# Fifteen instead of twelve gate halves queued among the banded steps of a hybrid decoder block

## The chip, the cores and the metric

The kernel runs on one core of a Trainium2 chip. The metric is the device time of one execution in microseconds. Engines are named as in the profile: PE (TensorE matmuls), PEld (its weight loads), DVE (VectorE), ACT (ScalarE), POOL (GpSimd) and SP (SyncE, which issues nearly all transfers here).

## The reference, cut to what matters

One decoder block on x of 1024 tokens by 1024 columns, in float32. Two attention branches work on the same normed input, each is weighted by a sigmoid gate, and their sum goes on through an output product and a squared-ReLU MLP.

```python
proj = jnp.einsum('bld,de->ble', h, w_in[l])
a_q, a_k, a_v, i_q, i_k, i_w, b_q, b_k, b_v, g_a, g_b = jnp.split(proj, offsets, axis=-1)
...
o_a = dsa_branch(a_q, a_k, a_v, i_q, i_k, i_w, topk)
...
o_b = swa_branch(b_q, b_k, b_v, sinks[l])
y_a = jnp.einsum('ble,ed->bld', o_a, w_branch_a[l])
y_b = jnp.einsum('ble,ed->bld', o_b, w_branch_b[l])
mix = jax.nn.sigmoid(g_a) * y_a + jax.nn.sigmoid(g_b) * y_b
x = x + jnp.einsum('bld,de->ble', mix, w_out[l])
```

The gate products are the columns g_a and g_b of the first product: 2048 columns for 1024 tokens. The sparse branch (o_a) keeps for each query the 256 keys with the highest index score; the banded branch (o_b) looks at the 128 latest keys, in two key blocks. Nothing in attention needs the gates; they are first read when the branches are mixed.

## The kernel before, in words

Products are made in float32r, each operand split into a rounded part and a remainder, so that a product is three matmuls (`mm3`, L111; lines L113 to L115). `split` (L101) makes the two parts: L104 on ACT or L106 on POOL rounds, L109 subtracts.

**Stages.** The input is loaded and three gates are made on the way (up to about 60 us). Then come the index keys and values, the index branch "i" (12 steps), the banded branch "b" (16 steps: two groups of heads by eight query blocks), the sparse branch "a" (16 steps, in the order of `A_STEPS`), the mix with the output product, and the MLP in two parts. Each branch runs through `pipeline` (L467), which writes out its steps one after the other. A step has four heads, in two parts: scores (L837), a reduction of them on DVE (L853), the exponential (L856), a division (L864 on POOL or L868 on DVE), transposes (L879), their split, the product with the values (L884, L885) and a copy (L892) that ends the step. The queries come from units, one for two query blocks: projection (tile mm, 48 matmuls of 256 columns), rotation (L436 to L442), split (`turned`, L444 to L456).

**The selection's search.** Which 256 keys a query keeps is found bit by bit: `bits` (L711) runs L676 on DVE for the three longest query blocks and L678 on ACT for three others, with small DVE operations between (L738 to L744). It is written among the banded steps and at the start of the sparse ones. `select` (L767 to L782) then turns the scores into a mask; it begins with L776 on DVE and L777 on POOL.

**The gates.** There are 16 gates of 128 columns, each in two halves of 512 tokens. A half is eight triples of matmuls into one bank (tile gt), a copy z on ACT (L292) and its store to memory (L293). `gates` (L300) makes them in order; a gate's weights come in two pieces of 128 by 512, loaded by SP and split on POOL (L106 and L109 with the tile of_h). There are two buffers for a piece as loaded, three for a split one, two gt banks and one buffer for z. Three gates are made at the start, so 13 gates, 26 halves, are left.

**Their place.** After each step, `finish` (L494) asks for as many halves as a digit of `FILL` says, and after the sparse branch all that are left are asked for (`fill(32)`, L948):

```python
fill(int(FILL[name][i:i + 1] or 0))
```

The digits for "i" are all 0, those for "b" sum to 12, those for "a" to 10; four halves are left for the end.

**What orders the work.** The program text gives each instruction a rank, but not its place in an engine's queue. The queues are written when the kernel is built (`schedule_with_timeline_sim`, L1424): a model of the engines is played through, and an engine takes, of what is ready then, the instruction with the earliest rank. On the chip each queue runs in the order so written and waits at an instruction whose inputs are not there. The lines that touch the change are L40 (`FILL`), L276 to L318 (`Gate`, `gates`, `fill`), L494 to L503 (`finish`) and L946 to L948.

Of the kernel before, what the change touches and what calls it, by code (L numbers as in the profile page):

```python
# [36 lines left out]
AKV = 10  # L37
EARLY = {'dve': 4, 'act': 3}
ZLATE = -6
FILL = {'i': '000000000000', 'b': '0222011001010101', 'a': '1111011010101010'}  # L40
PAIR = 0
W_AT = (2, 5)
AHEAD = {'i': (9, 4, 4), 'b': (6, 5, 4), 'a': (4, 4, 4)}
# [51 lines left out]
def decoder_block(tc, I, out):  # L95
# [220 lines left out]
    def fill(n):  # L316

        for _ in range(n):  # L318
            next(rest, None)
# [147 lines left out]
    def pipeline(name, steps, parts, begin=None, end=None, last=None, extra=()):  # L467
# [26 lines left out]
        def finish():  # L494
# [5 lines left out]
            if n + 1 == len(todo) or todo[n + 1][0] != i:  # L500
                if end:
                    end(i)
                fill(int(FILL[name][i:i + 1] or 0))  # L503

# [281 lines left out]
    def end(i):  # L786
        for kind in ("dve", "act"):
            if i == START[kind]:
                start(kind)
            if i > START[kind]:  # L790
                bits(kind, EARLY[kind])
# [636 lines left out]
```

## Time and profile before

| | us |
|---|---|
| three timed runs, median | 1459.85 |
| lowest and highest of them | 1451.63, 1462.02 |
| the profiled execution | 1455.47 |
| its span, first to last instruction | 1453.7 |

The profile shows one execution, the profiled one. Its times are counted from the span's start. An engine's busy time in a stretch is the sum of its instructions there; the ends of matmuls are modelled. The granted clock is TensorE's, as a share of its upper level.

### The profile page before, as it was taken

To read this page: it belongs to the slowest core of one execution; us is meant where nothing else is said; L and a number is where in the kernel's file an instruction comes from. 1 tells how busy PE (TensorE), PEld (TensorE's weight loads), DVE (VectorE), ACT (ScalarE), POOL (GpSimd) and SP (SyncE) were. 2 spreads that over 40 slices of the span, in tenths; PEclk is the share of its full clock that TensorE was granted. 3 is DMA by queue.
4 is the path that set the end of the run, shared out by engine and by line. 5 is a ranking of instruction groups with operands and counts; after the bars stand their busy time and mean duration, and the time that the engine had idled before them with its cause. 6 is when DMAs were issued, how large, how long until landed. Compare 5 with 4: busy or idle time off the path is not lost.

```text
span 1453.7 us, 21243 instructions
## 1 busy us (share of the span) xinstructions
PE 1374.5 (95%) x7096; PEld 1163.6 (80%) x7096; DVE 1080.2 (74%) x2115; ACT 779.0 (54%) x1612; POOL 461.4 (32%) x455
## 2 busy tenths in 40 slices
PE   8999997888898899789999999999999999999998
PEld 6989886677797788677878778888888888888887
DVE  8667799999889988776753586566664788687674
ACT  6335445666783547654445476555554545445453
POOL 4373865663758773323515310000000000001001
PEclk9999998999999999899999999999999999999999
DMA  7321231322433221456456465344443978643323
GB/s 267 111 74 48 79 108 58 88 76 57 108 84 88 53 71 29 116 165 207 153 166 174 131 212 204 141 150 149 159 146 110 333 251 310 211 119 93 109 74 116
DMA packets 135822, 196.10 MB, mean 135 GB/s; under 512 B 16032, under 2 KB 59168, under 8 KB 135584
## 3 DMA queue, kind: packets, MB, share of 16 engines
q1 hardware_dynamic: 135568, 194.74, 42.6%
q8 instruction: 56, 0.92, 0.3%
q14 instruction: 54, 0.44, 0.1%
q10 hardware_dynamic: 144, 0.00, 0.0%
HBM read 132.03 MB, written 55.84 MB: 129 GB/s over the span
## 4 chain that ended last, share of the span: by engine, by line
PE 62%; DVE 21%; DMA 5%; ACT 4%; issue 4%; POOL 3%; SPq 1%; DVEq 0%; ACTq 0%; POOLq 0%
PE pu L1121 7%; PE pu L1123 7%; PE pu L1122 7%; DVE of_a L676 7%; PE pdx L1320 4%; PE pdx L1318 4%; PE pdx L1319 4%; PE pdy L1320 3%; PE pdy L1318 3%; PE pdy L1319 3%; DVE wide L853 2%; PE pso L113 2%; PE pso L115 2%; PE pso L114 2%; DMA uall<-z_d 2%
## 5 line engine op out<-in xcount | busy, mean ns | idle before, releaser
L1265 POOL TENSOR_TENSOR y<-x,gf 128x512 f32<-128x512 f32 x4 | 6.3, 1601 | 492.9 <-DVE x L1249 491.5
L104 ACT ACTIVATE dao<-da 128x512 fp32r<-128x512 f32 x112 | 70.0, 630 | 132.1 <-PE pdx L1320 52.5
L856 ACT ACTIVATE wide<-wide,of_a 128x257 f32<-128x257 f32 (+9 forms) x128 | 81.0, 634 | 80.4 <-DVE of_a L853 79.4
L113 PE MATMUL mm<-of_h,of_w 128*128 128x256 f32 x416 | 119.6, 288 | 0.5 <-ACT of_g L292 0.5
L114 PE MATMUL mm<-of_h,of_w 128*128 128x256 f32 x416 | 118.9, 287 | 0.0
L115 PE MATMUL mm<-of_h,of_w 128*128 128x256 f32 x416 | 118.7, 287 | 0.1
L676 DVE TENSOR_SCALAR_CACHE_REDUCE of_a<-wide,of_a 128x768 bf16<-128x768 bf16 (+5 forms) x93 | 106.1, 1141 | 1.0
L109 DVE TENSOR_TENSOR dao<-da,dao 128x512 fp32r<-128x512 f32 x112 | 76.4, 686 | 36.8 <-ACT dao L104 36.6
L1121 PE MATMUL pu<-XT,uo 128*128 128x512 f32 x256 | 99.8, 390 | 0.8 <-ACT snap L1154 0.8
L1122 PE MATMUL pu<-XT,uo 128*128 128x512 f32 x256 | 99.6, 389 | 0.0
L1123 PE MATMUL pu<-XT,uo 128*128 128x512 f32 x256 | 99.5, 389 | 0.0
L113 PE MATMUL gt<-of_h 128*128 128x512 f32 x224 | 91.4, 408 | 6.6 <-ACT of_h L335 6.6
L1319 PE MATMUL pdx<-dbo,dao 128*128 128x512 f32 x248 | 94.9, 389 | 0.0
L1318 PE MATMUL pdx<-dbo,dao 128*128 128x512 f32 x248 | 94.8, 390 | 0.0
L115 PE MATMUL gt<-of_h 128*128 128x512 f32 x224 | 91.0, 408 | 2.5 <-POOL of_h L109 2.5
L1320 PE MATMUL pdx<-dbo,dao 128*128 128x512 f32 x248 | 93.0, 390 | 0.0
L678 ACT ACTIVATE of_a<-uall,of_a 128x384 int8<-128x384 f32 (+2 forms) x93 | 66.8, 719 | 48.7 <-DVE of_a L744 28.5
L114 PE MATMUL gt<-of_h 128*128 128x512 f32 x224 | 90.8, 405 | 0.5 <-DVE of_h L336 0.5
L837 PE MATMUL S<-of_w 128*128 128x256 f32 (+3 forms) x320 | 79.4, 342 | 11.9 <-DVE of_a L853 11.9
L879 PE MATMUL pt<-kept,wide 128*128 128x128 f32 x408 | 72.7, 283 | 14.0 <-DVE of_a L739 6.3
L113 PEld LDWEIGHTS mm<-of_h,of_w 128*128 128x128 f32 x416 | 80.5, 194 | 1.6 <-ACT of_g L292 0.7
L115 PEld LDWEIGHTS mm<-of_h,of_w 128*128 128x128 f32 x416 | 80.1, 193 | 1.4 <-POOL of_w L109 0.5
(284 smaller groups left out, 4315.0 us busy)
## 6 DMA issues: line engine op xcount, KB each, us to landing
u_d<-u SPq DMA_DIRECT2D x112, 256.0 KB, 2.2
da<-u_d SPq DMA_DIRECT2D x112, 256.0 KB, 2.9
ur<-in_w_up_dram SPq DMA_DIRECT2D x32, 512.0 KB, 4.9
dr<-in_w_down_dram SPq DMA_DIRECT2D x64, 256.0 KB, 5.3
z_d<-of_g SPq DMA_DIRECT2D x32, 256.0 KB, 2.2
uall<-z_d SPq DMA_DIRECT2D x32, 256.0 KB, 3.4
raw<-in_w_out_dram SPq DMA_DIRECT2D x32, 256.0 KB, 4.2
of_g<-in_w_g_dram SPq DMA_DIRECT2D x28, 256.0 KB, 2.8
```

The lines of the kernel that those rows point to most:

```text
L113: ins = nc.tensor.matmul(ps, lhsT=ah, rhs=bh, start=first, stop=False)
L114: nc.tensor.matmul(ps, lhsT=ah, rhs=bl, start=False, stop=False)
L115: nc.tensor.matmul(ps, lhsT=al, rhs=bh, start=False, stop=last)
L676: nc.vector.tensor_scalar(j, src, c, None, op0=ALU.is_lt, op1=ALU.add, accum_out=a)
L837: marks["S"] = nc.tensor.matmul(pS[:, :e - c], lhsT=st.unit(b, j), rhs=kT[:, a, k0 + c:k0 + e], start=a == 0, stop=a == 1).ins
L856: nc.scalar.activation(pe, pe, AF.Exp, bias=last, scale=-1.0, accum_out=st.sm[:, j:j + 1])
L1121: nc.tensor.matmul(ps, lhsT=ah, rhs=xh[:, at], start=f0, stop=False, skip_group_check=True)
L1122: nc.tensor.matmul(ps, lhsT=ah, rhs=xl[:, at], start=False, stop=False, skip_group_check=True)
L1123: nc.tensor.matmul(ps, lhsT=al, rhs=xh[:, at], start=False, stop=last, skip_group_check=True)
L1318: nc.tensor.matmul(ps, lhsT=ah[:, js], rhs=x[0][:, at], start=first, stop=False, skip_group_check=True)
L1319: nc.tensor.matmul(ps, lhsT=ah[:, js], rhs=x[1][:, at], start=False, stop=False, skip_group_check=True)
L1320: nc.tensor.matmul(ps, lhsT=al[:, js], rhs=x[0][:, at], start=False, stop=end, skip_group_check=True)
```

## The change

Three digits of the string for "b" change from 0 to 1; all others are the same. The banded steps 7, 8 and 12 (counted from 0) now ask for one half each. So fifteen halves stand among the banded steps, ten among the sparse ones as before, and one is left for the end in place of four. Every half from the ninth on stands earlier in the program than before.

```diff
-FILL = {'i': '000000000000', 'b': '0222011001010101', 'a': '1111011010101010'}
+FILL = {'i': '000000000000', 'b': '0222011111011101', 'a': '1111011010101010'}
```

## Rows read from the trace of the kernel before

**Rows 1.** The page, busy time and share of the span by engine.
```profile
PE 1374.5 (95%) x7096; PEld 1163.6 (80%) x7096; DVE 1080.2 (74%) x2115; ACT 779.0 (54%) x1612; POOL 461.4 (32%) x455
```

**Rows 2.** Busy time by stage, all engines: stretch, length, busy us (instructions), granted clock, DMA.
```profile
60.00:232.00 172.00, 163.99 (x1038) 148.52 (x1037) 136.55 (x237) 79.71 (x192) 105.21 (x87) 0.99 0.25 70
232.00:400.00 168.00, 140.23 (x859) 121.02 (x858) 159.32 (x462) 113.10 (x309) 94.25 (x134) 0.96 0.30 79
400.00:460.00 60.00, 58.90 (x429) 55.12 (x427) 51.26 (x136) 40.53 (x112) 43.57 (x43) 1.00 0.39 92
460.00:508.00 48.00, 39.88 (x249) 33.31 (x248) 47.20 (x119) 23.43 (x62) 33.65 (x38) 1.00 0.20 55
508.00:555.00 47.00, 46.61 (x265) 40.41 (x266) 37.46 (x78) 23.68 (x49) 32.36 (x25) 1.00 0.23 62
```

**Rows 3.** The same stages, the z copies alone (L292, one for each half).
```profile
60.00:232.00 172.00, 3.50 (x6) 0.99 0.25 70
232.00:400.00 168.00, 6.24 (x11) 0.96 0.30 79
400.00:460.00 60.00, 1.15 (x2) 1.00 0.39 92
460.00:508.00 48.00, 1.12 (x2) 1.00 0.20 55
508.00:555.00 47.00, 2.91 (x5) 1.00 0.23 62
```

**Rows 4.** The last of these stages, instructions on the gate tile alone.
```profile
508.00:555.00 47.00, 30.80 (x120) 21.60 (x120) 2.91 (x5) 1.00 0.23 62
```

**Rows 5.** Chain of waits from 508 to 555 us: shares, and its first gate piece.
```profile
by line: PE gt L113 19.7%; PE gt L114 19.5%; PE gt L115 19.5%; PE S L837 13.5%; PE pt L879 12.7%; PE pv L885 7.7%; PE pv L884 7.0%; DVE of_w L109 0.7%; DVE of_a L853 0.2%; issue 0.1%
...
508.78 0.23 PE gt L113
```

**Rows 6.** What DVE waited for from 508 to 555 us: us, times, longest.
```profile
DVE wide L853 <- PE S L837: 7.6, 5, 2.7
```

**Rows 7.** The same stages, the copies that end an attention step alone (L892).
```profile
60.00:232.00 172.00, 0.00 (x0) 0.99 0.25 70
232.00:400.00 168.00, 6.25 (x11) 0.96 0.30 79
400.00:460.00 60.00, 4.01 (x7) 1.00 0.39 92
460.00:508.00 48.00, 1.74 (x3) 1.00 0.20 55
508.00:555.00 47.00, 1.75 (x3) 1.00 0.23 62
```

**Rows 8.** Three of these stages, instructions on the projection tile alone.
```profile
400.00:460.00 60.00, 36.02 (x248) 32.70 (x248) 0.00 (x0) 2.87 (x5) 1.00 0.39 92
460.00:508.00 48.00, 12.81 (x85) 11.38 (x84) 0.00 (x0) 1.16 (x2) 1.00 0.20 55
508.00:555.00 47.00, 0.00 (x0) 0.00 (x0) 0.00 (x0) 0.59 (x1) 1.00 0.23 62
```

**Rows 9.** Groups of instructions on POOL from 160 to 560 us: the gate splits.
```profile
L109 POOL TENSOR_TENSOR of_h<-of_g,of_h 128x512 fp32r<-128x512 f32 x23 | 31.4, 1369 | 0.6
...
L106 POOL TENSOR_SCALAR of_h<-of_g 128x512 fp32r<-128x512 f32 x23 | 17.3, 755 | 13.1 <-PE gt L114 12.8
```

**Rows 10.** Chain of waits from 430 to 450 us: start, length, what.
```profile
434.27 1.71 POOL of_w L456
...
436.04 1.29 POOL of_h L109
...
440.50 1.29 POOL of_w L456
...
446.43 2.55 POOL uall L777
```

**Rows 11.** Line L738 on DVE: duration in ns, least, median and most.
```profile
L738 DVE TENSOR_TENSOR of_a<-of_a x31: 135/161/1287, 212.2 to 486.7; 128x3 f32<-128x3 f32 x31
```

## The prediction

> **What bounds the kernel now.** I read the page's busy line first, then one table by stage, then the tables that count finished work in the same stages, then waits and chain where the table pointed. The busy line has PE at 95% of the span and DVE at 74% [rows 1]. That is an average: the gate halves that the change moves run only up to 555 us, so only the stretches up to there matter.
>
> The stage table [rows 2] shows three kinds of stretch. From 232 to 400 us, where the banded steps run, DVE is busy 159.3 of 168 us (95%) and PE 140.2: DVE is the limit, and PE stands idle for 27.8 us. From 400 to 460 PE is full (58.9 of 60). From 460 to 508 it is DVE again (47.2 of 48), with 8.1 us of PE idle. From 508 to 555 PE is full (46.6 of 47), and DVE falls to 37.5, 9.5 us idle. In that last stretch five halves end [rows 3] and 120 gate matmuls run [rows 4]. The chain there is almost all PE, and the three gate lines make 19.7 + 19.5 + 19.5 = 58.7% of it, 27.6 us [rows 5]; each piece on it is 0.23 us, one matmul's pitch. DVE's waits in it are 7.6 us for a score product, five times [rows 6]: the sparse steps' scores stand behind gate products in PE's queue. So here gate work costs time, and in 232 to 400 PE would have room for it. That is the case for a gain.
>
> **What sets when a half runs.** The digits only say how early a half stands in the program. The count of z copies [rows 3] beside that of finished attention steps [rows 7] says whether halves wait for their place. Six halves end before 232 us, when no step of either branch has ended and the index branch's own digits are all 0. By 400 us 17 have ended, with 11 steps done. The old digits ask for 0+2+2+2+0+1+1+0+0+1+0 = 9 by then, the new ones for 11. By 460 us: 19 ended, 18 steps done (16 banded, 2 sparse), asked for 12 + 2 = 14 and now 17. By 508: 21 ended, 21 steps done, asked for 16 and now 19. By 555: all 26 ended, 24 steps done, asked for 18 and now 21. So halves already run ahead of their place, by eight at 400 us, and are still ahead of the new one everywhere. They are taken whenever the order written for PE had nothing with an earlier place to give it. A place that moves from 9 to 11 where 17 are done asks for nothing new.
>
> A new place can matter only against work that was ready at the same moment and stood between a half's old and new place. Up to 400 us the halves that run (the 7th to the 17th) stand behind every banded product that is then due, by either digits. From 400 to 460 it is otherwise: PE is full, and 248 of its matmuls are projections [rows 8], by then largely for sparse steps. Counting sparse steps from 0, the 18th half stood behind step 6 and now stands behind step 2, the 19th behind 8 and now 3, the 20th behind 10 and now 5. These can now go ahead of projections for later sparse steps.
>
> **The change part by part.** Nothing is added or removed: 26 queued halves before and after, with four left for the end before, one now.
>
> PE: a half is 8 x 3 = 24 matmuls of 0.228 us (0.23 in [rows 5]), 5.5 us; three are 16.4 us. Moved inside or between full stretches they exchange places with projections and cost nothing. One half displaces 48 matmuls of a projection (256 columns instead of 512, so an estimated 0.115 us each); what leaves 400 to 460 falls into 460 to 508. The bound on the good side: the displaced work fills the whole 8.1 us that PE has idle there, and 508 to 555 gets shorter by as much (DVE's 9.5 us idle would allow it): -8.1 us. The bound on the bad side is 0, since a projection has slack: the last of them run before 508, for steps that end after 555 [rows 7, 8]. I take 0, because PE's idle time there is time in which it stands at a product that waits for DVE, and gate products and projections were both at hand and did not fill it.
>
> ACT: three z copies of 0.58 us (2.91 / 5 in [rows 3]) move, 1.7 us; ACT is busy half of 460 to 508, and hides them. If not hidden, +1.7.
>
> DMA: three weight loads and three z stores of 256 KB move past others in SP's queue. SP stands behind nothing that PE wants at once: loads run a weight buffer ahead, and the DMA engines are busy 20 to 39% of each stage [rows 2]. Cost 0; bound +2.1 us, one weight piece that comes late by as long as its split takes [rows 9].
>
> POOL: each half needs half a gate's weight, one piece, split on POOL: 0.755 + 1.369 = 2.12 us [rows 9]. Three pieces are 6.4 us. From 400 to 460 POOL is busy 43.6 of 60 us, and from 433 to 449 the chain is POOL alone: a rotation (L456), a gate split (L109 of_h), then the scaling that a selection waits for (L777) [rows 10]. A split that has an earlier place goes ahead of these. Bounds: 0 if the pieces fall behind 449, +6.4 if all three stand in front on that chain. I take 0: two pieces already run in that stretch, splits wait for PE to give a weight buffer back (12.8 us of POOL's idle time, [rows 9]), and what POOL loses there it does not have to do in 508 to 555.
>
> POOL's work can also hold up DVE. The 128x3 operation of L738 takes 161 ns in the median and 1287 ns at most [rows 11], about one POOL split. The Trainium skill, page SBUF — State Buffer, section SBUF: two separate sides, says that DVE and GpSimd share a port pair under an exclusive lock, and that a DVE operation with two SBUF inputs is fully blocked while a GpSimd instruction holds it; the row agrees. By that rule each piece that moves into a DVE-full stretch costs DVE up to its length, and the sum would be +6.4 us for three. The sum below takes 0 for it, for the pieces leave a stretch in which they hold up DVE as well.
>
> Sum: PE 0, ACT 0, DMA 0, POOL 0, so no change on the profiled execution, 1455.47 us (span 1453.7 and 1.8 around it). The three timed runs have a median of 1459.85 (1451.63 to 1462.02); the mean of these four executions is 1457.2. I predict 1457 us. A measurement of this kernel tells about 1% (14.6 us) from no change.
>
> **Rivals.** (A) The halves do go where the digits put them: by 400 us 19 or 20 have ended instead of 17. For it: 27.8 us of idle PE there. Against it: the counts, which never wait for the digits. Three halves (16.4 us) leave 508 to 555, where DVE's idle time caps the gain: -9.5, 1447.7 us.
>
> (B) Slower, by POOL from 430 to 450: the splits of the 18th to 20th half stand in front of the rotation and of the selection's scaling, and the sparse branch starts later. For it: the chain is on POOL there and has a gate split in it [rows 10]. Against it: PE full at the same time. It decides once more than the two pieces of before run from 400 to 449. Price 2.12 to 6.4 us, so up to 1463.6; if DVE is also held up for their length from 460 to 508, as its operation was in [rows 11], 12.8, so 1470.
>
> (C) The order that is written for the queues is another one throughout, because a few places changed: all shifts are then possible. By the idle times, PE's 8.1 and DVE's 9.5 together, down to -17.6; up, to the whole 16.4 us of gate products standing in front of DVE's scores without being won back later.
>
> **How the numbers follow.** No change within 5 us: 0.52. (A): 0.22. (B): 0.17. (C): 0.09, shared between both signs. The range runs from (A) less the spread of single runs (some 4 us) to (B) and part of (C): 1444 to 1473; the forecast's own is 1452 to 1462. Faster by over 1% needs all of (A) and a low run, or (C): a third of 0.22 and half of 0.09, 0.12. Slower by over 1% needs (B) at its upper price and a high run, or (C): 0.12. The rest, 0.76, is within 1%.
>
> **What would show it.** In the changed kernel's profile: z copies before 400 us stay at 17 (one more or less), and the banded steps end at the same times. From 400 to 508 one to three halves more have ended, and fewer than five end after 508. The stretch in which PE is full and DVE waits for scores ends within 5 us of 555. POOL's chain at 433 to 449 keeps its length. It is wrong if by 400 us 19 or more halves have ended and the sparse branch ends over 8 us earlier (A), or if the first selection's scaling starts over 4 us later than at 446 us with more gate splits before it (B).

## The result, and the profile after

| | us |
|---|---|
| kernel before, median of 12 runs | 1454.36 (1450.10 to 1462.02) |
| changed kernel, median of 12 runs | 1462.99 (1461.87 to 1467.58) |
| ratio | 1.0053, 95% interval 1.0041 to 1.0065 |
| profiled execution, changed kernel | 1467.58, span 1465.8 |

The change costs 0.53%, about 8 us. The profiled execution of the changed kernel is its slowest of the twelve, 4.6 us above the median, so the two spans differ by more (12.1 us) than the kernels do. Part of that is one execution's clock, which shows where the work is still the same: written out, PE's two queues are the same up to about 412 us, yet the stage from 232 to 400 has 142.58 us of PE for 857 matmuls here and had 140.23 for 859 before [rows 2], at a granted clock of 0.95 against 0.96.

The page's busy line of the changed kernel, which answers to [rows 1]:

```profile
PE 1381.6 (94%) x7096; PEld 1169.4 (80%) x7096; DVE 1083.0 (74%) x2115; ACT 781.6 (53%) x1612; POOL 464.4 (32%) x455
```

The instructions are the same in number, but PE's 7096 matmuls take 7.1 us longer than in [rows 1]. The stages of [rows 2] in the changed kernel, all engines:

```profile
60.00:232.00 172.00, 163.92 (x1036) 148.74 (x1036) 135.14 (x239) 77.92 (x188) 103.32 (x86) 0.98 0.25 71
232.00:400.00 168.00, 142.58 (x857) 123.02 (x855) 159.25 (x460) 114.79 (x311) 95.05 (x134) 0.95 0.29 77
400.00:460.00 60.00, 52.91 (x367) 49.04 (x368) 49.59 (x134) 40.43 (x112) 36.18 (x38) 0.96 0.39 97
460.00:508.00 48.00, 43.41 (x248) 36.98 (x247) 45.33 (x114) 21.25 (x56) 34.73 (x38) 0.94 0.21 57
508.00:555.00 47.00, 42.11 (x252) 36.73 (x251) 37.49 (x69) 19.67 (x43) 38.33 (x28) 0.96 0.19 47
```

Up to 400 us nothing has moved but for a lower clock. From 400 to 460 PE is no longer full: 7.1 us idle instead of 1.1. From 460 to 508 it is idle for less (4.6 instead of 8.1), and from 508 to 555 for 4.9 instead of 0.4. None of these stages is left in which PE is full. The granted clock, 1.00 in all three of these stages before, is 0.96, 0.94 and 0.96: part of each is at the lower of its two levels (1.2 and 2.4 GHz). From 440 to 460, in the kernel before and in the changed one:

```profile
440.00:460.00 20.00, 20.00 (x124) 17.72 (x122) 19.17 (x39) 4.95 (x11) 18.87 (x15) 1.00 0.38 91
```

```profile
440.00:460.00 20.00, 15.54 (x88) 13.78 (x87) 15.07 (x39) 8.29 (x19) 9.85 (x10) 0.88 0.29 67
```

PE was busy throughout at a granted clock of 1.00, and now stands idle for 4.5 us and has 0.88.

Finished halves in the same stages (z copies, L292), as in [rows 3]:

```profile
60.00:232.00 172.00, 3.50 (x6) 0.98 0.25 71
232.00:400.00 168.00, 6.25 (x11) 0.95 0.29 77
400.00:460.00 60.00, 1.16 (x2) 0.96 0.39 97
460.00:508.00 48.00, 1.72 (x3) 0.94 0.21 57
508.00:555.00 47.00, 1.15 (x2) 0.96 0.19 47
```

By 400 us 17 halves have ended, as before, and by 508 one more than before. Two more end after 555. Projections, in turn, run late: from 508 to 555 there were none [rows 8], now there are 76 matmuls (the projection tile alone):

```profile
508.00:555.00 47.00, 10.58 (x76) 9.86 (x76) 0.00 (x0) 1.15 (x2) 0.96 0.19 47
```

PE runs the same 7096 matmuls in all kernels of this study, so its idle time can serve as a ledger, though not a complete one. From 400 to 760 us, where the sparse branch and the mix end, the kernel before:

```profile
400.00:760.00 360.00, 331.34 (x1881) 282.33 (x1880) 283.62 (x600) 200.54 (x416) 184.32 (x165) 0.97 0.40 113
```

and the changed one:

```profile
400.00:760.00 360.00, 324.36 (x1826) 276.27 (x1827) 283.31 (x601) 196.38 (x409) 187.25 (x167) 0.96 0.38 110
```

360 less the first number is 28.7 us of idle PE before and 35.6 after: 7.0 us more. Before 400 us the same difference is 42.9 and 41.6. So the idle time is lost behind 400 us, in the part of the queues that was written anew. It is not the whole account: over the whole span PE is idle for 79.2 us before and 84.2 after, 5.0 more, and the other 7.1 of the 12.1 us between the two spans are the same matmuls at a lower clock (mean 0.986 before and 0.980 after). No run takes idle time and clock apart.

### The profile page after: what moved, and what is told of

The parts are those of the page before. It is cut to its first block, busy times and chain, and to the rows that moved or that the text cites. A ratio compares the mean times of both kernels' runs of the same rounds, so it can differ in the third digit from the quotient of the medians.

```text
span 1465.8 us, 21177 instructions
## 1 busy us (share of the span) xinstructions
PE 1381.6 (94%) x7096; PEld 1169.4 (80%) x7096; DVE 1083.0 (74%) x2115; ACT 781.6 (53%) x1612; POOL 464.4 (32%) x455
## 4 chain that ended last, share of the span: by engine, by line
PE 63%; DVE 22%; issue 4%; ACT 4%; DMA 4%; POOL 2%; SPq 1%; DVEq 0%; ACTq 0%; POOLq 0%
PE pu L1123 7%; PE pu L1121 7%; PE pu L1122 7%; DVE of_a L676 7%; PE pdx L1320 4%; PE pdx L1318 4%; PE pdx L1319 4%; PE pdy L1320 3%; PE pdy L1318 3%; PE pdy L1319 3%; DVE wide L853 2%; PE psy L113 2%; PE psy L114 2%; PE psy L115 2%; DVE of_w L109 2%
## 5 line engine op out<-in xcount | busy, mean ns | idle before, releaser
L113 PE MATMUL mm<-of_h,of_w 128*128 128x256 f32 x416 | 121.5, 293 | 0.0
L114 PE MATMUL mm<-of_h,of_w 128*128 128x256 f32 x416 | 121.2, 292 | 0.0
L115 PE MATMUL mm<-of_h,of_w 128*128 128x256 f32 x416 | 120.8, 292 | 0.1
L109 DVE TENSOR_TENSOR dao<-da,dao 128x512 fp32r<-128x512 f32 x112 | 76.3, 687 | 43.0 <-ACT dao L104 42.9
L678 ACT ACTIVATE of_a<-uall,of_a 128x384 int8<-128x384 f32 (+2 forms) x93 | 66.8, 718 | 49.6 <-DVE of_a L744 29.0
L837 PE MATMUL S<-of_w 128*128 128x256 f32 (+3 forms) x320 | 79.2, 341 | 13.8 <-DVE of_a L853 13.8
L114 PEld LDWEIGHTS mm<-of_h,of_w 128*128 128x128 f32 x416 | 82.6, 199 | 1.0
L113 PEld LDWEIGHTS mm<-of_h,of_w 128*128 128x128 f32 x416 | 82.6, 199 | 1.0
```

Source lines behind the costliest of these rows:

```text
L109: (nc.gpsimd if l_on == "pool" else nc.vector).tensor_tensor(l, src, f(h), ALU.subtract)
L113: ins = nc.tensor.matmul(ps, lhsT=ah, rhs=bh, start=first, stop=False)
L114: nc.tensor.matmul(ps, lhsT=ah, rhs=bl, start=False, stop=False)
L115: nc.tensor.matmul(ps, lhsT=al, rhs=bh, start=False, stop=last)
```

## The experiments

All ratios are to the kernel before on the same chip, three rounds each. The expectations speak of these theories: that the 18th and later halves now stand in front of sparse projections on PE (T1, later "the early halves"); that any new written order has a time of its own (T2); a cost among the banded steps (T3); POOL's queue, where splits stand in front of a rotation or of the selection's scaling L777 (T4, "POOL theory"); PE's order alone (T5, "PE theory").

The table has what the runs gave. "18th" is when the 18th half's copy starts, "search" the time from the first to the last start of L678 from 400 to 447 us (18 operations in each kernel, the same six bits of the search on ACT), "idle" PE's idle time from 400 to 760. Each of the last three is read from one profiled execution; before and e2, whose queues are the same, differ by 1.4 us in the last.

| kernel | ratio, interval | 18th | search | idle |
|---|---|---|---|---|
| before | 1 | 444.0 | 36.4 | 28.7 |
| changed | 1.0053 [1.0041, 1.0065] | 432.1 | 41.2 | 35.6 |
| e2, only places 9 to 15 moved | 0.9999 [0.9984, 1.0013] | 444.7 | 36.4 | 30.1 |
| e3, 13 halves | 1.0029 [1.0015, 1.0044] | 444.5 | 36.3 | 32.3 |
| e4, 14 halves | 1.0033 [1.0019, 1.0047] | 440.9 | 34.8 | 33.5 |
| e10, 16 halves | 1.0057 [1.0035, 1.0079] | 426.0 | 36.3 | 35.7 |
| q3, 11 halves | 1.0022 [1.0007, 1.0037] | 444.3 | 36.3 | 31.2 |
| q4, 9 halves | 1.0022 [1.0009, 1.0035] | 445.2 | 36.3 | 33.1 |
| p1, before, scaling on ACT | 1.0101 [1.0084, 1.0118] | 444.3 | 36.4 | 40.8 |
| p2, changed, scaling on ACT | 0.9999 [0.9985, 1.0014] | 430.1 | 40.8 | 31.1 |
| p3, before, late splits off POOL | 1.0037 [1.0022, 1.0052] | 444.4 | 36.3 | 31.7 |
| p4, changed, late splits off POOL | 1.0045 [1.0028, 1.0063] | 431.4 | 41.0 | 35.4 |
| q1, changed, late splits behind scaling | 1.0059 [1.0040, 1.0079] | 431.8 | 40.7 | 38.4 |
| q2, before, the same | 1.0022 [1.0006, 1.0038] | 444.6 | 36.2 | 27.4 |
| r1, only up to the 18th moved | 1.0057 [1.0039, 1.0075] | 431.7 | 40.7 | 35.1 |
| r2, up to the 19th | 1.0051 [1.0032, 1.0071] | 429.6 | 40.6 | 34.2 |
| r3, up to the 20th | 1.0084 [1.0064, 1.0105] | 432.6 | 40.4 | 39.4 |
| r4, only the 20th and later | 1.0007 [0.9993, 1.0022] | 446.1 | 36.2 | 30.4 |
| t1, changed, 18th held | 1.0063 [1.0042, 1.0085] | 437.8 | 39.6 | 36.3 |
| t2, before, 18th held | 1.0036 [1.0022, 1.0049] | 445.3 | 38.5 | 28.2 |

**How many, and which places.** The first runs change digits alone.

```diff
-'b': '0222011001010101', 'a': '1111011010101010'
+'b': '0222011111011101', 'a': '0001011010101010'   e2
+'b': '0222011101010101', 'a': '1111011010101010'   e3
+'b': '0222011111010101', 'a': '1111011010101010'   e4
+'b': '0222011111111101', 'a': '1111011010101010'   e10
```

> Fifteen halves among the banded steps as in the changed kernel, but the sparse digits cut so that the 16th half and all behind it keep the places they had before. Theory T1 (what counts is the place of the 18th and later halves against projections of the sparse branch; up to 400 us halves run ahead of any place): ratio to before 1.000, within 0.2%, z copies and steps at the times of before. Theory T3 (the three halves cost where the digits put them, among the banded steps): about 1.005, as the changed kernel.

> Thirteen halves among the banded steps instead of twelve, so that every half from the ninth on is one place earlier. T1: the loss grows with the number of places; a third of 7.7 us, +2 to +3 us (1.001 to 1.002). T2 (each new written order has a time of its own, without regard to the number): any value from -8 to +8 us.

> Fourteen instead of twelve. T1: +4 to +6 us (1.003 to 1.004), between thirteen and fifteen. T2: out of order with thirteen and fifteen.

> Sixteen instead of twelve. T1: at least the loss of fifteen, +8 to +12 us (1.005 to 1.008). T2: as likely below fifteen as above.

e2 has the changed digits among the banded steps, with all places from the 16th half on as before. Written out, its queues are those of the kernel before on every engine, and its time is the same. A kernel whose three extra halves all stand at the last banded step was written out too, and had the changed kernel's queues. So the digits within the banded steps do nothing (T3 falls), and all of the loss is in the places of the 16th half and later. One, two, three and four halves more cost 0.29, 0.33, 0.53 and 0.57%, which is the order of T1; but e3 is above T1's 1.001 to 1.002, and its 18th half ends when it did before, so what e3 costs is not T1's cause.

**POOL's queue.** The changed kernel's chain of waits from 508 us has the following, with start, length and what ran:

```profile
507.95 2.36 POOL of_a L442
510.31 0.59 POOL of_h L106
510.89 1.28 POOL of_w L109
512.17 0.71 POOL wide L864 x2
512.88 1.87 POOL uall L777
```

A gate split and one of the sparse projections' last weights stand in front of the scaling of 128x640, which before started at 501.1. It is the fourth of the six to start; the expectations call it the fifth. DVE's waits from 508 to 555 say the same; they were for scores alone [rows 6]:

```profile
DVE uall L779 <- POOL uall L777: 4.4, 2, 3.9
DVE wide L853 <- PE S L837: 2.3, 1, 2.3
```

So the next runs took the scaling off POOL (p1, p2; to fit in memory the later tile sq has one buffer instead of two in both), or these late splits (p3, p4), or held the splits behind a scaling (q1, q2).

```diff
-        nc.gpsimd.tensor_scalar(s, s, sgn[:, b:b + 1], None, op0=ALU.mult)
+        nc.scalar.activation(s, s, AF.Copy, scale=sgn[:, b:b + 1])         p1, p2
-    more = Columns(I["w_aq"][0], 2, 256, "pool", "pool", tag="p")
+    more = Columns(I["w_aq"][0], 2, 256, "act", "dve", tag="p")            p3, p4
+    def behind(k, plain=more.load):                                        q1, q2
+        with tc.issue_after(marks["scaled", 5]): return plain(k)
+    more.load = behind
```

> The kernel before, with the scaling that opens a selection (L777) on ACT instead of POOL, and one buffer instead of two for the last stage's squares (the memory asks for it). Theory T4 (the loss is POOL's queue: splits of weights that come later stand in front of the selection's scaling and of rotations): 0.995 to 1.001 against before, since six scalings of 2.7 us leave POOL and ACT is busy half of 460 to 555 us. T5 (PE's order alone costs, POOL is only where it shows): 1.000.

> The changed kernel with the same two edits, to be compared with the run before it. T4: the distance to that run shrinks from 7.7 us to 3 us or less. T5: it stays at 6 to 9 us.

> The kernel before, with the four last pieces of projection weights split on ACT and DVE instead of POOL. T4: 1.000 to 1.002 (they are done by 463 us there; DVE takes on four subtractions of 0.7 us, 2.7 us at most, in a stretch where it is full). T5: the same.

> The changed kernel with the same edit: the four pieces that POOL splits from 489 to 512 us, in front of the scalings, go to ACT and DVE. T4: distance to the run before it 4 us or less, and the third to fifth scaling start 3 to 8 us earlier than in the changed kernel. T5: distance 6 to 9 us.

> The changed kernel, with the last pieces of the sparse projections' weights (tile of_w, lines L106 and L109 on POOL) written no earlier than the fifth scaling of a selection's scores (L777), so that they cannot stand in front of it. POOL theory (splits in front of the scaling cost the time): that scaling starts before 505 us (512.9 in the changed kernel), DVE's waits for L777 between 496 and 556 us fall from 6.3 us to under 2, and the ratio to the kernel before is 0.999 to 1.003. PE theory (the order of gate products and projections on PE alone): 1.005, as the changed kernel. Theory of a new written order with a time of its own: any value, with no link to the fifth scaling's start.

> The kernel before with the same edit, the control. In the kernel before these pieces were done by 463 us, 38 us ahead of the fifth scaling (501.1), so the edit makes them late there and takes nothing out of its way. POOL theory: 1.000 to 1.003, as the projections that need the pieces have slack. PE theory: 1.000 to 1.003 too, unless a projection stands at its late weights. Theory of a new written order: any value.

p2 gave the whole loss back. But p1, the same edit on the kernel before, was 1.0% slower where T4 expected at most 0.1%, and p2 came out 15.3 us below p1, where T4 expected 3 us or less between them and T5 6 to 9: it is an edit that gains half a per cent in one order and loses one in another. p4 is 1.5 us above p3, as T4 had it, yet mostly because p3 lost: it is above T4's 1.002.

q1 was to be the test without that doubt, but its edit does less than its expectation says. The mark `marks["scaled", 5]` is the scaling of block 5, counted from 0, which is that of 128x768 and the third to start (493.3 us in q1). The 128x640 scaling is that of block 4 and comes after it, and five of POOL's operations on these weights still ran in between. That scaling in the changed kernel:

```profile
L777 POOL TENSOR_SCALAR uall<-uall,of_a x1: 1884/1884/1884, 512.9 to 512.9; 128x640 f32<-128x640 f32 x1
```

and that of q1:

```profile
L777 POOL TENSOR_SCALAR uall<-uall,of_a x1: 1887/1887/1887, 509.0 to 509.0; 128x640 f32<-128x640 f32 x1
```

It started 3.9 us earlier, at 509.0 where T4 wanted less than 505; DVE's waits for L777 from 496 to 556 us fell from 6.3 to 3.5, not under 2; and the time stayed at 1.0059. So q1 alone does not settle T4. The other traces do: DVE's waits for L777 from 440 to 560 us are 7.7 us in the changed kernel, 1.4 in p4, 2.4 in r1 and 2.1 in r3 (both below), and the last three stand at 1.0045, 1.0057 and 1.0084; r4 waits for 3.7 at 1.0007 and q2 for 5.7 at 1.0022. The wait for POOL was real, but the time does not follow it.

**Fewer halves.** If an earlier place costs, a later one might gain.

```diff
-'b': '0222011001010101'
+'b': '0222011001010100'   q3
+'b': '0222011001000000'   q4
```

> The kernel before with eleven instead of twelve halves among the banded steps (the last digit 1 of b becomes 0). If the number of halves that may go ahead of the sparse projections sets the time (+1, +2, +3 and +4 halves gave 1.0029, 1.0033, 1.0053 and 1.0057), one fewer gives 0.996 to 1.001, not slower than before. Theory of a new written order with a time of its own: any value, as likely above 1.002 as below 0.998.

> The kernel before with nine halves among the banded steps (its last three digits 1 become 0). By the number of halves: 0.992 to 1.001. Theory of a new written order: any value.

Neither gains: both are at 1.0022, and with q2 and p3 that makes four new orders with no half earlier than before that cost 0.22 to 0.37%. T2 has half of this right: a new order has a time of its own, and part of any ratio here may be owed to that alone. That none of the orders tried beats that of the kernel before, T2 did not say. In these the 18th half still ends at 444 to 445 us, whether it is asked for at sparse step 6, 8 or 12. So a later place does not hold a half back, as little as an earlier one moved those before 400.

**Early places against late ones.** r1 to r3 bring the places up to the 18th, the 19th and the 20th half forward, the last of them to where the change has it, and keep the later ones at the old places (those up to the 17th have ended by 400 us anyway). r4 keeps all up to the 19th and moves those behind, the 20th and 21st not quite as far as the change does (step 8 in place of 5 and 6), the 22nd to 25th as it does.

```diff
-'a': '1111011010101010'
+'a': '2220000010101010'   r1
+'a': '2221000000101010'   r2
+'a': '4111010000001010'   r3
+'a': '1111011040101010'   r4
```

> The kernel before with only the 16th to 18th half moved, to where the change puts the 18th (the 18th from sparse step 6 to 2; the 19th and all later ones at their old places). PE's written queue is that of the changed kernel up to its row 2228 (the order leaves that of before at row 2086, about 412 us). Theory of the early halves (a half taken ahead of the sparse projections from 412 us on leaves PE without ready work before 460): PE idle from 400 to 460 us is 5 to 8 us (1.1 before, 7.1 changed), ratio 1.003 to 1.006. Theory of the later halves: ratio 0.999 to 1.002. Theory that any new order costs: 1.002 to 1.004, with PE idle there as it may be.

> The same with the 19th half moved too (from step 8 to 3), the 20th and later at their old places; PE's queue is the changed kernel's up to row 2316. Theory of the early halves: PE idle from 400 to 460 us 5 to 8 us, ratio 1.004 to 1.006, not less than with the 18th alone. Theory of the later halves: 0.999 to 1.002. Any new order: 1.002 to 1.004.

> The same with the 18th, 19th and 20th half moved (the 20th from step 10 to 5), the 21st and later at their old places; PE's queue is the changed kernel's up to row 2315. Theory of the early halves: as the changed kernel, ratio 1.004 to 1.006, PE idle from 400 to 460 us 5 to 8 us. Theory of the later halves: 0.999 to 1.002. Any new order: 1.002 to 1.004.

> The other part alone: the 18th half stays at its old place (step 6) and the 19th at step 8, the 20th to 22nd come to step 8, the 23rd to 25th to steps 10, 12 and 14 as the change has them. PE's queue is that of before up to row 2363 (some 40 us later than where the change first differs). Theory of the early halves: PE idle from 400 to 460 us stays near 1 us, ratio 0.999 to 1.002. Theory of the later halves: 1.004 to 1.006. Any new order: 1.002 to 1.004.

This splits the loss most clearly: moved up to the 18th, 1.0057; the later ones alone, 1.0007, within its interval no change. The two intervals do not touch. The expectations of PE's idle time from 400 to 460 failed in part: it is 3.4 us in r1 and 4.3 in r2, not 5 to 8, and in r1 it comes later (9.0 from 460 to 508); in r4 it is 2.1, not near 1. And r3, at 1.0084, is above every theory's range. From 400 to 760 r1's adds up to the changed kernel's, 35.1 and 35.6. How much of r1's 0.57% is owed to the early places is open: orders with no half earlier than before cost up to 0.37% (p3). In r1 and r4, the stretch is:

```profile
400.00:760.00 360.00, 324.85 (x1843) 277.65 (x1844) 283.04 (x600) 196.54 (x409) 188.74 (x167) 0.96 0.39 110
```

```profile
400.00:760.00 360.00, 329.58 (x1868) 282.64 (x1869) 284.59 (x605) 199.60 (x414) 186.64 (x168) 0.96 0.39 111
```

**Is it the 18th half in front of the projections at 412 us?** There the orders part. The gate tile alone from 412 to 424 us and from 436 to 448, in the kernel before:

```profile
412.00:424.00 12.00, 3.07 (x11) 1.85 (x11) 0.00 (x0) 1.00 0.31 76
436.00:448.00 12.00, 2.46 (x10) 1.81 (x10) 0.59 (x1) 1.00 0.56 134
```

and in the changed kernel:

```profile
412.00:424.00 12.00, 5.07 (x19) 3.37 (x19) 0.00 (x0) 1.00 0.44 116
436.00:448.00 12.00, 6.38 (x24) 4.23 (x24) 0.60 (x1) 1.00 0.36 83
```

Eight gate matmuls more, and by the projection tile's rows 28 projection matmuls there in place of 45. The last two kernels hold that half back.

```diff
-                gate.half(half)
+                with tc.issue_after(marks["mm"]) if len(asked) == 17 else nullcontext(): gate.half(half)
+                asked.append(half)
```

> The changed kernel, all its digits, with one thing more: the matmuls of the 18th half are queued on PE behind the last projection matmul that the program has reached when it asks for that half. PE's written queue is then that of the kernel before at row 2086, where the change first differs, and leaves it at row 2132 only. Theory of the early halves (the 18th half in front of the sparse projections from 412 us on is the cost): 0.999 to 1.003, and 11 or fewer gate matmuls instead of 19 from 412 to 424 us. Theory that the change's digits cost in another way: 1.004 to 1.006. Any new order: 1.002 to 1.004.

> The kernel before with the same hold of the 18th half (which it asks for four sparse steps later), so that it stands behind still more projections. Theory of the early halves: not slower than before by more than 0.2%, and faster if the 11 gate matmuls that the kernel before has from 412 to 424 us cost it something too: 0.997 to 1.002. Any new order: 1.002 to 1.004.

In t1 the hold did what it should at 412, and the time stayed at 1.0063; that narrow form falls. The same two stretches in t1:

```profile
412.00:424.00 12.00, 0.00 (x0) 0.00 (x0) 0.00 (x0) 1.00 0.39 100
436.00:448.00 12.00, 6.48 (x24) 4.15 (x24) 1.15 (x2) 1.00 0.35 90
```

Held to 424, the 18th half ran right after and the 19th behind it, so that by 448 two whole halves had run, as in the changed kernel, and one in the kernel before. What was tested is the stretch to 424 us and not the one to 448. t2, the same hold in the kernel before, came out at 1.0036, above the 0.997 to 1.002 of that theory and within what any new order was said to cost; its 18th half ends when it did before, and its search is 2.1 us longer.

**What the early halves hold up.** The search shows it. L678 on ACT in the kernel before, over the same six bits, with duration in ns (least, median, most) and first and last start:

```profile
L678 ACT ACTIVATE of_a<-uall,of_a x18: 605/717/834, 401.0 to 437.4; 128x384 int8<-128x384 f32 x6, 128x512 int8<-128x512 f32 x6, 128x640 int8<-128x640 f32 x6
```

in the changed kernel:

```profile
L678 ACT ACTIVATE of_a<-uall,of_a x18: 602/712/835, 403.3 to 444.5; 128x384 int8<-128x384 f32 x6, 128x512 int8<-128x512 f32 x6, 128x640 int8<-128x640 f32 x6
```

and in r4:

```profile
L678 ACT ACTIVATE of_a<-uall,of_a x18: 603/714/835, 403.4 to 439.6; 128x384 int8<-128x384 f32 x6, 128x512 int8<-128x512 f32 x6, 128x640 int8<-128x640 f32 x6
```

The operations are as long as ever; the last one comes 41.2 us after the first instead of 36.4 or 36.2. The changed kernel's chain of waits from 425 to 447 us says where most of the 4.8 us went:

```profile
425.00 0.47 ACT of_a L436
...
427.37 1.99 DMA of_a<-of_a
...
429.48 0.69 DVE of_a L441
430.17 1.19 DVE of_a L744
...
433.75 2.03 DMA of_a<-of_a
...
435.90 0.69 DVE of_a L441
...
436.62 1.67 DVE of_w L456
...
438.83 0.63 DVE of_a L741
...
439.69 1.15 DVE of_a L744
```

A projection's result is copied (L436), SP sends it over (the transfer lands 2 us later), DVE rotates it (L441) and splits it (L456), and only then come the search's small operations (L741, L744), which stand behind these in DVE's queue. That a queue waits as a whole is also in the Trainium skill, page PSUM — Partial Sum Buffer, section Engine vs sequencer instructions, which calls the queues of ScalarE, VectorE and GpSimdE strictly first in, first out; this chain agrees, with L741 at 438.83 behind the split that began at 436.62. L744, one for each bit, starts at 423.2, 430.1 and 439.7 here; in the kernel before it was 421.6, 426.3 and 433.0. In the bit from 430.1 to 439.7 the search stands in DVE's queue behind a rotation and a split: ACT's last L678 ended at 436.33, and L741 came 2.4 us later. In the kernel before, DVE's queue in the same bit was:

```profile
431.72 0.17 DVE L741 TENSOR_TENSOR of_a<-of_a 128x3 int32<-128x3 f32 x1 [0.72 <-ACT of_a L678]
...
432.24 0.68 DVE L456 TENSOR_TENSOR of_w<-of_a,of_w 64x512 fp32r<-64x512 f32 x1
432.96 1.26 DVE L744 TENSOR_SCALAR of_a<-of_a 128x3 int32<-128x3 int32 x1
434.13 0.68 DVE L441 TENSOR_TENSOR of_a<-of_a 128x512 f32<-128x512 f32 x1
```

There DVE stood waiting for ACT's L678, and the split and the rotation came behind L741. Over the six bits the time from the end of the last L678 to L741 sums to 3.9 us here and 0.9 before, 3.0 of the 4.8 us; most of the rest is ACT's own queue, where other copies and exponentials stand between the L678. That DVE's order came out so because PE made a gate half first is a reading, not shown. The first scaling follows, at 451.9 instead of 446.4.

By the table all kernels but four fall into two groups by this: search 36.2 to 36.4 us, ratio 0.9999 to 1.0037 (e2, e3, p3, q2, q3, q4, r4); search 38.5 to 41.2, ratio 1.0036 to 1.0084 (the changed one, p4, q1, r1, r2, r3, t1, t2). The four: e4 has the shortest search (34.8) at 1.0033, e10 loses 0.57% with an unhindered search, p1 loses 1.0% with one, and p2 loses nothing with a late one. r1 against r4 shows that the late search comes with the early places, but t2, in which no half is earlier, has 2.1 us of it too. That it is the cause of the loss, or the whole of it, is not shown, and those four speak against it: p2 has the same late search as the changed kernel (40.8) and no loss. No run held the search's place in DVE's queue alone, so that link is read from the trace. What the idle column adds is a ledger, not a cause. In the changed kernel PE's waits from 400 to 508 us are for DVE, 11.6 us, but for 0.4 for POOL.

## Why the prediction was wrong

The forecast was no change, 1457 us, and the measured change is 0.53%, outside what the interval allows for none, though within the 1% that the text counted as no change. By its steps:

- **When a half runs: right up to 400 us, and right on where to look.** 17 halves by 400, the same number of finished steps, and only from 400 us on can a place change anything. One half more ended by 508 and four after it, as its signs had it. e2 shows it best: with the places from the 16th on kept, the queues are the same.
- **Rival (A): wrong**, as the text weighed it; nothing went into the idle PE of 232 to 400.
- **The term of PE: the step that failed.** "The bound on the bad side is 0, since a projection has slack: the last of them run before 508, for steps that end after 555". Slack was read off the last projections; what those from 412 on feed (rotation, split) shares DVE's queue with the search, and in the order that was written it stands in front of it. Moving places up to the 18th half alone costs 0.57% (r1), 8.3 us of 1455.7, where the term was bounded by 0. The later ones, of which the sentence was true, cost nothing that can be told (r4). The term also left out PE's clock: the same matmuls took 7.1 us longer in the profile, some of it that execution's own. That moving the places has a price, which the term put at 0, is shown; through which wait the time was lost, and how much of it any new order would have cost, stays open. (Its estimate of 0.115 us for a projection matmul is low too: [rows 8] has 36.02 us for 248, 0.145.)
- **The terms of ACT and DMA: 0.** No wait of PE for a z copy appears in the changed kernel's waits from 400 to 508, and DMA's share is as before. No run took them apart.
- **The term of POOL, and rival (B): the sign right, the mechanism not.** The first scaling was 5.5 us late, over the 4 that were to be the mark of (B); but 2.3 of that is the profiled execution's own lateness at 400 us. And (B) wanted more than two gate pieces on POOL from 400 to 449, and there were two, as before. The scaling was late because the search ended late. Splits did stand in front of a scaling, 60 us further on, and p4, which took those of the projections' weights off POOL, won at most a little (1.0045 against 1.0053, the intervals overlap). That the price of (B), 1463.6, is near the measured 1463.0 is chance.
- **The rule on DVE and POOL from the Trainium skill**, page SBUF — State Buffer, section SBUF: two separate sides, would have made it +6.4 us. The runs neither bear that out nor exclude it: DVE's busy time from 400 to 760 us is 283.62 before and 283.31 after, so no longer operations show in sum. A single one does: DVE's split at 436.62, in the chain above, took 1.67 us, and its like in the kernel before (432.24) 0.68; POOL's rotation L441 ran from 435.94 to 437.74.
- **The full stretch up to 555: wrong.** DVE's waits for scores fell from 7.6 us [rows 6] to 2.3, as fewer halves stood there, and it brought nothing: DVE then waited for the scaling instead (4.4 us), and PE had late projections to make.
- **Rival (C), a new order throughout,** was given 0.09 with both signs. The runs make it larger and of one sign: every new order but r4 and p2 was slower, by 0.22 to 1.01%.

## What to carry to other kernels

Filler work that is moved up costs nothing only if what it passes has slack at that very place; read the slack from the first consumer of the displaced work, through every queue that runs in order, and not from when the last of its kind ends. In a schedule that is written out by a model, a small change of places rewrites the whole order behind it: compare against several edits that should do nothing, before a few tenths of a per cent are put down to a cause, and test a cause by an edit in both kernels, since one that helps in one order can hurt in the other. Where a hold or a mark is part of the edit, look in the trace whether the work stands where it was to stand: q1 ran without that being so. And when PE's idle time is the ledger, put its busy time and granted clock beside it.

## What was not expected

- The same edit, the scaling on ACT, gains about 0.5% on the changed kernel (1.0053 to 0.9999) and loses 1.0% on the kernel before. In the latter PE then stood for a score product behind DVE for 7.1 us at one time.
- Of 17 further written orders none was faster than the one of before beyond its interval; the best, r4 and p2, are equal to it.
- Two profiled executions with the same queues on all engines (before and e2) have PE busy for 1374.5 and 1370.9 us with the same 7096 matmuls. A difference of 4 us in PE's busy time between single profiles is no evidence here, and the 7.1 us above is one such difference. Over all executions the three slowest kernels, p1, r3 and t1, have mean granted clocks of 0.977 to 0.985, and the kernel before 0.980 to 0.991.
